# Modulation rows taken in pairs, and queued behind weight products in the first two mixers

## The chip, the cores and the metric

The kernel runs on one core of a Trainium2 chip. The metric is the device time of one execution in microseconds (us); the kernel before takes 1922.84 us, the median of three runs (1920.18 to 1924.93).

## The reference

Four layers run over 256 tokens of width 1024. The first two ("block 1") have a mixer (differential attention with a gated recurrence in the first, dilated attention in the second), a layer norm, a 4096-wide squared-ReLU network and a gate. The last two ("block 2") take the same tokens as a denoising stream beside 256 context tokens: their mixer joins gated linear attention, neighbourhood attention and sliding-window attention. Both are scaled, shifted and gated by six modulation rows for each of the two layers and each of two conditioning vectors. In short, for layer `l`:

```
m = silu([c_2, c_ctx_2]) @ w_mod_2[l] + b_mod_2[l]     # 2 x 6*1024, from 1024 x 6*1024 weights
x = x + m[2] * mixer(rms(x) * (1 + m[1]) + m[0])
x = x + m[5] * ffn  (rms(x) * (1 + m[4]) + m[3])
```

All is float32. The two modulation products read 2 x 25 MB of weights for two rows of output each. They depend on the two conditioning vectors alone, so they can be computed at any time before block 2 uses them.

## The kernel before, in words

Weights stream from HBM on SyncE's queue (SP) in units of up to 512 KB. A unit lands in one of four buffers `wr` (line 212), ScalarE copies it to a rounded high part `wh` (L214) and VectorE takes the rest `wl` (L216). TensorE then makes three products for each weight block: high by high, high by low, low by high (L279 to L281 in projections, L825 to L827 and L850 to L852 in block 1's network, L1473 to L1475 and L1499 to L1501 in block 2's). Each of these is called a weight product here. Units are consumed in the order in which the program names them.

The modulation weights go another way. `modulation(l, box, js)` (L938) makes four parts for each of the six rows `j`; a part `u` covers two blocks of 128 weight rows, `k = 2u` and `2u + 1`. For each block it loads 128 x 1024 numbers (512 KB, L955, SP) into a buffer `raw`, and multiplies them unsplit (L957): `cT`, 128 x 32, is the stationary side, and four products of 256 columns each write one of four groups of 32 partitions of the PSUM tile `fil`, each on its own column group of the array. TensorE runs a float32 product in two passes, so that a block of weight rows has 8 matmul records and a part has 16. In this text a block of weight rows is a **row**, and a part's two rows are a **pair**. VectorE then adds the four groups to `bm` (L959). There is one PSUM buffer `fil`, and there are two buffers for the rows, tag `fr` (the first six rows use `bc`). A row's buffer is free for the next load when its products are done. The whole program has 12 x 4 = 48 pairs.

The list of program items is woven by hand: modulation parts stand between the items of both mixers of block 1 (`mod(0, 0)` to `mod(0, 2)` in the first, `mod(0, 5)` and `mod(1, 0)` in the second), beside the first block of their networks (`mod(0, 3)`, `mod(1, 1)`), in the second network (`mod(0, 4)`), and in block 2. The order on each engine is not that of the list, however. A planner with a timeline of its own goes through the instructions: when an engine comes free in that timeline, the earliest in the list that is ready is queued next, with some evacuations brought forward by `tc.high_priority`. So modulation products can be queued ahead of weight products that stand earlier in the list but aren't ready in the planner's timeline, and other work that becomes ready can be queued between the products of a pair. On the chip each engine takes its queue strictly in that order.

Of the kernel before, what the change touches and what calls it, by code (L numbers as in the profile page):

```python
# [119 lines left out]
def body(ctx: ExitStack, tc: tile.TileContext, A: dict, out: bass.AP):  # L120
# [29 lines left out]

    mm = nc.tensor.matmul
    V = nc.vector
    S = nc.scalar
# [114 lines left out]
    def proj(w, kdim, chunks, xs, evac, t_outer=(), tag="acc", first=0):  # L268
# [6 lines left out]
        def mms(o, x, wt, u):  # L275
            (xh, xl), (wh, wl) = x, wt
            for kk in range(2):
                k = 2 * ((u + first) % nu) + kk
                mm(o, xh[:, k, :], wh[:, kk, :], start=(u == 0 and kk == 0), stop=False)  # L279
                mm(o, xh[:, k, :], wl[:, kk, :], start=False, stop=False)  # L280
                mm(o, xl[:, k, :], wh[:, kk, :], start=False, stop=(u == nu - 1 and kk == 1))  # L281

# [27 lines left out]
    def projT(w, kdim, c0, nb, xs, evac, tag="acc"):  # L310
# [4 lines left out]
        def part(wt, u):  # L315
            (wh, wl), xT = wt, xs.box["T"].both
            if u == 0:
                held.extend(new((P, 2, 256)) for _ in range((nb + 1) // 2))
            for kk in range(2):
                k = 2 * u + kk  # L320
                mh, ml = [m[:, k, :] for m in xT]
                for b in range(nb):
                    o = held[b // 2][:, b % 2, :]
                    bs = slice(b * P, (b + 1) * P)
                    mm(o, wh[:, kk, bs], mh, start=(k == 0 and b % 2 == 0), stop=False, skip_group_check=True)
                    mm(o, wh[:, kk, bs], ml, start=False, stop=False, skip_group_check=True)
                    mm(o, wl[:, kk, bs], mh, start=False, stop=(k == kdim - 1), skip_group_check=True)
            if 2 * u == kdim - 2:
                evac(held)
# [459 lines left out]
    def block1_layer(l, xT, done, side):  # L789
# [25 lines left out]
        def up_part(g, u, wt):  # L815
# [3 lines left out]
            for b in range(4):  # L819
                o = pss[g][b // 2][:, b % 2, :]  # L820
                for kk in range(2):
# [4 lines left out]
                    mm(o, wh[:, kk, bs], ml, start=False, stop=False, skip_group_check=True)  # L826
                    mm(o, wl[:, kk, bs], mh, start=False, stop=(k == 7), skip_group_check=True)  # L827
            if u == 3:
# [9 lines left out]
        def down_part(g, hs, *us):  # L838
# [3 lines left out]
            for t in range(2):  # L842
                ts_ = slice(t * P, (t + 1) * P)
                for n in range(2):
                    o = acc[g][t][n]
                    for i, h in enumerate(hs):
                        wh, wl = us[2 * i + n]
                        for kk in range(2):
                            b = 2 * h + kk
                            mm(o, hh[:, b, ts_], wh[:, kk, :], start=(b == 0), stop=False)  # L850
                            mm(o, hh[:, b, ts_], wl[:, kk, :], start=False, stop=False)  # L851
                            mm(o, hl[:, b, ts_], wh[:, kk, :], start=False, stop=(b == 3))  # L852
                    if 1 in hs:
# [83 lines left out]

    def modulation(l, box, js):  # L938

        st = {}  # L940

        def part(j, u):
# [3 lines left out]
            if u == 0:  # L946
                bm = st[j] = T([P, 256], F32, "gate" if j in (2, 5) else "bm", 3 if j in (2, 5) else 1)
                V.memset(bm, 0.0)
                for s in range(2):
                    nc.sync.dma_start(bm[s:P:32, :], A["b_mod_2"][l, j * D:(j + 1) * D].rearrange("(g n) -> g n", g=4))  # L950
            bm, ps = st[j], PT("fil")
            for k in (2 * u, 2 * u + 1):
                early[0] += 1
                raw = T([P, D], F32, "bc" if early[0] <= 6 else "fr", 2)
                nc.sync.dma_start(raw, A["w_mod_2"][l, k * P:(k + 1) * P, j * D:(j + 1) * D])  # L955
                for g in range(4):
                    mm(ps[32 * g:32 * g + 32, 0:256], cT[:, k, :], raw[:, 256 * g:256 * g + 256],  # L957
                       start=(k == 2 * u), stop=(k == 2 * u + 1), tile_position=(0, 32 * g))
            V.tensor_tensor(bm, ps[:, 0:256], bm, ALU.add)  # L959
# [458 lines left out]
    def block2_layer(l, xT, pr, box, ce, done, side):  # L1418
# [44 lines left out]
        def up_part(g, m, u, wt):  # L1463
# [3 lines left out]
            for b in range(2):  # L1467
                o = pss[g][m][:, b, :]
                bs = slice(b * P, (b + 1) * P)
                for kk in range(4):  # L1470
# [3 lines left out]
                    mm(o, wh[:, kk, bs], ml, start=False, stop=False, skip_group_check=True)  # L1474
                    mm(o, wl[:, kk, bs], mh, start=False, stop=(k == 7), skip_group_check=True)  # L1475
            if m == 1 and u == 1:
# [8 lines left out]
        def down_part(gs, *us):  # L1485
# [5 lines left out]
            for t in range(2):  # L1491
                ts_ = slice(t * P, (t + 1) * P)
                for n in range(2):
                    cs = slice(n * 512, (n + 1) * 512)
                    o = acc["y"][t][n]
                    for i, (g, (hh, hl)) in enumerate(zip(gs, hs)):
                        wh, wl = us[2 * i + n]
                        for kk in range(2):
                            mm(o, hh[:, kk, ts_], wh[:, kk, :], start=(kk == 0 and g == 0), stop=False)  # L1499
                            mm(o, hh[:, kk, ts_], wl[:, kk, :], start=False, stop=False)  # L1500
                            mm(o, hl[:, kk, ts_], wh[:, kk, :], start=False, stop=(kk == 1 and g == NG - 1))  # L1501
                    if NG - 1 in gs:
# [22 lines left out]
    def ctx_ffn(box):  # L1525
# [16 lines left out]
        def up_part(g, m, u, wt):  # L1542
# [3 lines left out]
            for b in range(2):  # L1546
                o = pss[g, m][:, b, :]
                bs = slice(b * P, (b + 1) * P)
                for kk in range(4):
# [3 lines left out]
                    mm(o, wh[:, kk, bs], ml, start=False, stop=False, skip_group_check=True)  # L1553
                    mm(o, wl[:, kk, bs], mh, start=False, stop=(k == 7), skip_group_check=True)
            if u == 0:
# [11 lines left out]
        def down_part(g, *us):  # L1567
# [3 lines left out]
            for t in range(2):  # L1571
                ts_ = slice(t * P, (t + 1) * P)
                for n in range(2):
# [3 lines left out]
                    for kk in range(2):  # L1577
                        mm(o, h[:, 0, kk, ts_], wh[:, kk, :], start=(kk == 0), stop=False)
                        mm(o, h[:, 0, kk, ts_], wl[:, kk, :], start=False, stop=False)
                        mm(o, h[:, 1, kk, ts_], wh[:, kk, :], start=False, stop=(kk == 1))  # L1580
                    if g == 0:
# [79 lines left out]
    program = [do(begin)]  # L1661
    def mod(l, *js):
        return modulation(l, boxes[l], js)

    program += block1_layer(0, xTs[0], to_next(1), dict(tail=flat(ctx_a[:1]), lr=4, mix=mod(0, 0, 1) + ctx_n + mod(0, 2), first=flat(ctx_a[1:2]) + mod(0, 3),
                                                        ffn=ctx_a[2:-2], end=flat(ctx_a[-2:]), last=[]))
    program += block1_layer(1, xTs[1], to_next(2), dict(tail=[], lr=6, mix=mod(0, 5) + mod(1, 0), first=mod(1, 1),
                                                        ffn=weave(ctx_b[:-2], mod(0, 4)), end=flat(ctx_b[-2:]), last=[]))
# [60 lines left out]
```

## Time and profile before

| | us |
|---|---|
| median of three runs | 1922.84 |
| profiled execution | 1921.25 |
| its span | 1919.10 |
| TensorE busy | 1844.6 (96%) |
| VectorE busy | 1224.0 (64%) |
| ScalarE busy | 988.6 (52%) |
| modulation products (L957), union of their time | 64.96 |

The profile's timeline gives an instruction's start, its duration, engine (PE is TensorE, DVE VectorE, ACT ScalarE), line, operands and shape, and how many alike follow each other; in brackets stands the idle time before it and what ended it. `128*32` are the active rows and columns of the array. Matmuls are pipelined, so that the distance of two starts, not the duration, is what one costs. A row of the windows view has the stretch, its length, the busy time with the number of instructions for PE, PEld (weight loads), DVE, ACT and POOL, then the granted TensorE clock as a share of full speed, the mean share of time that the DMA engines were busy, and GB/s. A row of the waits view has who waited, for whom, the total us, how often, and the longest. A row of the chain of waits has start, us, and what the time went to.

### The profile page before, as it was taken

How to read it: one execution, taken by the hardware profiler on the slowest of the kernel's cores; microseconds unless marked ns; L12 is line 12 of the kernel's file. 1: busy time of each engine (PE TensorE's matmuls, PEld its weight loads, DVE VectorE, ACT ScalarE, POOL GpSimd, SP SyncE). 2: the span in 40 equal slices, each digit the busy share in tenths (PEclk: the TensorE clock that was granted, in tenths of full speed). 3: DMA queues.
4: the chain of work that ended last, by engine and by line, in shares of the span. 5: the costliest groups of instructions: out<-in, count | busy, mean ns of one | idle time of the engine just before them, and what ended most of it. 6: DMA issues, size and time to landing. Idle time of an engine off the chain costs nothing. (4 is left out here: it accounts for less than half of the span.)

```text
span 1919.1 us, 31908 instructions
## 1 busy us (share of the span) xinstructions
PE 1844.6 (96%) x12481; PEld 1576.3 (82%) x12481; DVE 1224.0 (64%) x2333; ACT 988.6 (52%) x1630; POOL 50.8 (3%) x74
## 2 busy tenths in 40 slices
PE   7999999999999899999899999999999999989997
PEld 5766888997887688888787889899898886669997
DVE  5565656656676666668577876685646666755555
ACT  5453564544565364544568553454546556344443
POOL 1000000000000000000000000000000000000000
PEclk9999999999999899999899999999999999989999
DMA  8645654545656554465353355556665464456553
GB/s 279 250 165 189 231 183 150 178 156 192 214 171 198 192 188 150 169 220 175 118 170 104 122 162 168 168 181 193 195 212 166 156 187 146 141 176 185 182 183 98
DMA packets 100835, 338.84 MB, mean 177 GB/s; under 512 B 11572, under 2 KB 12812, under 8 KB 100684
## 3 DMA queue, kind: packets, MB, share of 16 engines
q1 hardware_dynamic: 100140, 336.43, 54.5%
q8 instruction: 98, 1.61, 0.4%
q0 software_dynamic: 544, 0.36, 0.2%
q14 instruction: 53, 0.43, 0.1%
HBM read 335.70 MB, written 1.05 MB: 175 GB/s over the span
## 5 line engine op out<-in xcount | busy, mean ns | idle before, releaser
L216 DVE TENSOR_TENSOR wl<-wr,wh 128x1024 fp32r<-128x1024 f32 (+3 forms) x562 | 637.6, 1137 | 412.8 <-ACT wh L214 406.3
L214 ACT CAST wh<-wr 128x1024 fp32r<-128x1024 f32 (+3 forms) x562 | 549.6, 981 | 655.2 <-PE acc L281 132.0
L279 PE MATMUL acc<-wh,mh 128*128 128x256 f32 (+3 forms) x400 | 132.3, 336 | 3.5 <-ACT mh L378 2.0
L280 PE MATMUL acc<-wl,mh 128*128 128x256 f32 (+3 forms) x400 | 130.8, 329 | 0.7 <-DVE wl L216 0.7
L281 PE MATMUL acc<-wh,ml 128*128 128x256 f32 (+3 forms) x400 | 131.1, 330 | 0.0
L279 PE MATMUL acc<-wh,xh 128*128 128x512 f32 (+3 forms) x304 | 117.4, 396 | 6.0 <-ACT xh L378 3.8
L280 PE MATMUL acc<-wl,xh 128*128 128x512 f32 (+3 forms) x304 | 118.6, 390 | 1.7 <-DVE wl L216 1.7
L281 PE MATMUL acc<-wh,xl 128*128 128x512 f32 (+3 forms) x304 | 117.8, 388 | 0.1
L850 PE MATMUL acc<-wh,a 128*128 128x512 f32 x256 | 101.8, 401 | 0.0
L851 PE MATMUL acc<-wl,a 128*128 128x512 f32 x256 | 101.5, 396 | 0.0
L852 PE MATMUL acc<-wh,a 128*128 128x512 f32 x256 | 101.0, 396 | 0.0
L1473 PE MATMUL sc<-xh,wh 128*128 128x256 f32 x352 | 99.7, 284 | 0.5 <-ACT xh L378 0.5
L1474 PE MATMUL sc<-xl,wh 128*128 128x256 f32 x352 | 99.7, 283 | 0.0
L1475 PE MATMUL sc<-xh,wl 128*128 128x256 f32 x352 | 99.5, 283 | 0.0
L1474 PE MATMUL sc<-ml,wh 128*128 128x256 f32 x352 | 99.1, 282 | 0.0
L1473 PE MATMUL sc<-mh,wh 128*128 128x256 f32 x352 | 98.9, 281 | 0.0
L1475 PE MATMUL sc<-mh,wl 128*128 128x256 f32 x352 | 98.4, 280 | 0.0
L279 PEld LDWEIGHTS acc<-wh,mh 128*128 128x128 f32 x400 | 75.3, 189 | 14.2 <-issue 3.2
L280 PEld LDWEIGHTS acc<-wl,mh 128*128 128x128 f32 x400 | 75.8, 189 | 6.6 <-DVE wl L216 1.2
L281 PEld LDWEIGHTS acc<-wh,ml 128*128 128x128 f32 x400 | 75.5, 189 | 6.7 <-issue 0.6
L279 PEld LDWEIGHTS acc<-wh,xh 128*128 128x128 f32 x304 | 58.4, 194 | 22.4 <-ACT xh L378 4.5
L825 PE MATMUL sc<-mh,wh 128*128 128x256 f32 x256 | 74.6, 292 | 1.4 <-DVE ml L358 1.4
(571 smaller groups left out, 4687.1 us busy)
## 6 DMA issues: line engine op xcount, KB each, us to landing
wr<-in_ffn_w_dram SPq DMA_DIRECT2D x128, 512.0 KB
fr<-in_w_mod_dram SPq DMA_DIRECT2D x90, 512.0 KB
wr<-in_w_gate_dram SPq DMA_DIRECT2D x66, 512.0 KB
wr<-in_w_up_dram SPq DMA_DIRECT2D x66, 512.0 KB
wr<-in_w_down_dram SPq DMA_DIRECT2D x66, 512.0 KB
wr<-in_w_in_dram SPq DMA_DIRECT2D x40, 384.0 KB
wr<-in_ev_w_in_dram SPq DMA_DIRECT2D x28, 512.0 KB
wr<-in_w_in_dram SPq DMA_DIRECT2D x28, 512.0 KB
```

The lines of the kernel that those rows point to most:

```text
L214: S.copy(hi, raw)
L216: V.tensor_tensor(lo, raw, hi, ALU.subtract)
L279: mm(o, xh[:, k, :], wh[:, kk, :], start=(u == 0 and kk == 0), stop=False)
L280: mm(o, xh[:, k, :], wl[:, kk, :], start=False, stop=False)
L281: mm(o, xl[:, k, :], wh[:, kk, :], start=False, stop=(u == nu - 1 and kk == 1))
L825: mm(o, wh[:, kk, bs], mh, start=(k == 0 and b % 2 == 0), stop=False, skip_group_check=True)
L850: mm(o, hh[:, b, ts_], wh[:, kk, :], start=(b == 0), stop=False)
L851: mm(o, hh[:, b, ts_], wl[:, kk, :], start=False, stop=False)
L852: mm(o, hl[:, b, ts_], wh[:, kk, :], start=False, stop=(b == 3))
L1473: mm(o, wh[:, kk, bs], mh, start=(k == 0 and b == 0), stop=False, skip_group_check=True)
L1474: mm(o, wh[:, kk, bs], ml, start=False, stop=False, skip_group_check=True)
L1475: mm(o, wl[:, kk, bs], mh, start=False, stop=(k == 7), skip_group_check=True)
```

## The change

`modulation` gets a flag `hold`. A part first allocates and loads both rows of its pair, and then issues its eight products: first each column group with one row (groups 0 and 2 with the second row, 1 and 3 with the first), then each with the other row. With `hold`, the eight products get an edge to the weight product that was traced last before them: TensorE's queue has them behind it, without a wait for its end. `wm` records that product, the third of each triple. All parts of `mod(0, 0)` to `mod(0, 3)`, `mod(0, 5)`, `mod(1, 0)` and `mod(1, 1)` are held (28 pairs); those of `mod(0, 4)` and `mod(1, 2)` to `mod(1, 5)` are not (20 pairs). The row loads, buffers, the number of products and the add on VectorE stay as they are.

```
+    dense = []
+    def wm(*args, **kw):
+        dense[:] = [mm(*args, **kw).ins]
...
-                mm(o, xl[:, k, :], wh[:, kk, :], start=False, stop=(u == nu - 1 and kk == 1))
+                wm(o, xl[:, k, :], wh[:, kk, :], start=False, stop=(u == nu - 1 and kk == 1))
...
-    def modulation(l, box, js):
+    def modulation(l, box, js, hold):
...
+            raws = {}
             for k in (2 * u, 2 * u + 1):
                 early[0] += 1
-                raw = T([P, D], F32, "bc" if early[0] <= 6 else "fr", 2)
-                nc.sync.dma_start(raw, A["w_mod_2"][l, k * P:(k + 1) * P, j * D:(j + 1) * D])
-                for g in range(4):
-                    mm(ps[32 * g:32 * g + 32, 0:256], cT[:, k, :], raw[:, 256 * g:256 * g + 256],
-                       start=(k == 2 * u), stop=(k == 2 * u + 1), tile_position=(0, 32 * g))
+                raws[k] = T([P, D], F32, "bc" if early[0] <= 6 else "fr", 2)
+                nc.sync.dma_start(raws[k], A["w_mod_2"][l, k * P:(k + 1) * P, j * D:(j + 1) * D])
+            with tc.issue_after(dense[0]) if hold and dense else nullcontext():
+                for rnd in range(2):
+                    for g in range(4):
+                        k = 2 * u + (g + rnd + 1) % 2
+                        mm(ps[32 * g:32 * g + 32, 0:256], cT[:, k, :], raws[k][:, 256 * g:256 * g + 256],
+                           start=(k % 2 != g % 2), stop=(k % 2 == g % 2), tile_position=(0, 32 * g))
...
-    program += block1_layer(0, ..., mix=mod(0, 0, 1) + ctx_n + mod(0, 2), first=flat(ctx_a[1:2]) + mod(0, 3), ...
+    program += block1_layer(0, ..., mix=mod(0, 0, 1, hold=True) + ctx_n + mod(0, 2, hold=True), first=flat(ctx_a[1:2]) + mod(0, 3, hold=True), ...
-    program += block1_layer(1, ..., mix=mod(0, 5) + mod(1, 0), first=mod(1, 1), ...
+    program += block1_layer(1, ..., mix=mod(0, 5, hold=True) + mod(1, 0, hold=True), first=mod(1, 1, hold=True), ...
```

The other lines that change from `mm` to `wm` are the third products of the other triples.

## Rows read from the trace of the kernel before

**Rows 1.** The page, part 1: busy time of each engine.
```profile
PE 1844.6 (96%) x12481; PEld 1576.3 (82%) x12481; DVE 1224.0 (64%) x2333; ACT 988.6 (52%) x1630; POOL 50.8 (3%) x74
```

**Rows 2.** Windows over the two mixers of block 1.
```profile
25.00:60.00 35.00, 31.78 (x185) 21.75 (x178) 20.75 (x30) 25.79 (x29) 0.53 (x1) 1.00 0.80 284
...
135.00:162.00 27.00, 24.79 (x178) 16.18 (x177) 15.00 (x45) 8.34 (x25) 0.00 (x0) 0.87 0.69 227
162.00:212.00 50.00, 49.55 (x264) 36.68 (x262) 35.97 (x54) 23.64 (x41) 5.05 (x5) 1.00 0.63 215
...
545.00:615.00 70.00, 68.42 (x562) 53.73 (x561) 47.71 (x200) 40.62 (x117) 0.00 (x0) 0.98 0.64 207
```

**Rows 3.** Source view of line 957, rows in buffers fr: ns min/median/max.
```profile
L957 PE MATMUL fil<-fr,cT x720: 376/379/637, 57.7 to 1867.1; 128*32 128x256 f32 x180
```

**Rows 4.** Timeline of TensorE around a pair taken at once.
```profile
480.17 0.39 PE L281 MATMUL acc<-wh,xl 128*128 128x512 f32 x1
480.49 1.07 PE L957 MATMUL fil<-fr,cT 128*32 128x256 f32 x16
481.49 0.74 PE L279 MATMUL acc<-wh,xh 128*128 128x512 f32 x2
482.07 0.40 PE L280 MATMUL acc<-wl,xh 128*128 128x512 f32 x1
```

**Rows 5.** Timeline of TensorE around a single row.
```profile
42.26 0.39 PE L279 MATMUL acc<-wh,xh 128*128 128x512 f32 x1
42.58 0.64 PE L957 MATMUL fil<-bc,cT 128*32 128x256 f32 x8
43.15 0.50 PE L280 MATMUL acc<-wl,xh 128*128 128x512 f32 x1
43.48 0.39 PE L281 MATMUL acc<-wh,xl 128*128 128x512 f32 x1
```

**Rows 6.** Timeline of TensorE around one product, a quarter of a row.
```profile
645.01 0.39 PE L281 MATMUL acc<-wh,xl 128*128 128x512 f32 x1
645.33 0.62 PE L957 MATMUL fil<-fr,cT 128*32 128x256 f32 x2
645.88 0.50 PE L279 MATMUL acc<-wh,t 128*128 128x512 f32 x1
646.21 0.39 PE L280 MATMUL acc<-wl,t 128*128 128x512 f32 x1
```

**Rows 7.** Timeline of TensorE, further modulation products.
```profile
155.89 1.08 PE L957 MATMUL fil<-fr,cT 128*32 128x256 f32 x8
...
579.26 1.07 PE L957 MATMUL fil<-fr,cT 128*32 128x256 f32 x16
...
596.89 0.62 PE L957 MATMUL fil<-fr,cT 128*32 128x256 f32 x2
```

**Rows 8.** TensorE's waits for modulation rows: 0:212, 466:646 and 1600:1730 us.
```profile
PE fil L957 <- DMA fr<-in_w_mod_dram: 1.0, 1, 1.0
...
PE fil L957 <- DMA fr<-in_w_mod_dram: 1.1, 1, 1.1
...
PE fil L957 <- DMA fr<-in_w_mod_dram: 8.5, 6, 2.9
```

**Rows 9.** Waits of SyncE's queue, the whole span.
```profile
SPq L212 <- DVE wl L216: 1149.4, 432, 18.6
SPq L955 <- PE fil L957: 110.3, 54, 7.9
```

**Rows 10.** Chain of waits in the last layer: a row's landing.
```profile
1702.45 4.73 DMA fr<-in_w_mod_dram
```

**Rows 11.** Timeline of TensorE: the second row of that pair.
```profile
1709.09 1.08 PE L957 MATMUL fil<-fr,cT 128*32 128x256 f32 x8 [0.69 <-DMA fr<-in_w_mod_dram]
```

**Rows 12.** Timelines of VectorE and TensorE at the first layer norm.
```profile
203.72 1.41 DVE L403 SCALAR_TENSOR_TENSOR x<-x,stb,bc 128x512 f32<-128x512 f32 x2
...
206.59 0.66 PE L177 MATMUL sc<-ident,x 128*128 128x128 f32 x4
```

More of the change, by code (lines that the diff above doesn't have):

```diff
@@ L1 @@
 import math
+from contextlib import nullcontext
 from contextlib import ExitStack
@@ L326, in part @@
                     mm(o, wh[:, kk, bs], ml, start=False, stop=False, skip_group_check=True)
-                    mm(o, wl[:, kk, bs], mh, start=False, stop=(k == kdim - 1), skip_group_check=True)
+                    wm(o, wl[:, kk, bs], mh, start=False, stop=(k == kdim - 1), skip_group_check=True)
             if 2 * u == kdim - 2:
@@ L826, in up_part @@
                     mm(o, wh[:, kk, bs], ml, start=False, stop=False, skip_group_check=True)
-                    mm(o, wl[:, kk, bs], mh, start=False, stop=(k == 7), skip_group_check=True)
+                    wm(o, wl[:, kk, bs], mh, start=False, stop=(k == 7), skip_group_check=True)
             if u == 3:
@@ L851, in down_part @@
                             mm(o, hh[:, b, ts_], wl[:, kk, :], start=False, stop=False)
-                            mm(o, hl[:, b, ts_], wh[:, kk, :], start=False, stop=(b == 3))
+                            wm(o, hl[:, b, ts_], wh[:, kk, :], start=False, stop=(b == 3))
                     if 1 in hs:
@@ L1474, in up_part @@
                     mm(o, wh[:, kk, bs], ml, start=False, stop=False, skip_group_check=True)
-                    mm(o, wl[:, kk, bs], mh, start=False, stop=(k == 7), skip_group_check=True)
+                    wm(o, wl[:, kk, bs], mh, start=False, stop=(k == 7), skip_group_check=True)
             if m == 1 and u == 1:
@@ L1500, in down_part @@
                             mm(o, hh[:, kk, ts_], wl[:, kk, :], start=False, stop=False)
-                            mm(o, hl[:, kk, ts_], wh[:, kk, :], start=False, stop=(kk == 1 and g == NG - 1))
+                            wm(o, hl[:, kk, ts_], wh[:, kk, :], start=False, stop=(kk == 1 and g == NG - 1))
                     if NG - 1 in gs:
@@ L1553, in up_part @@
                     mm(o, wh[:, kk, bs], ml, start=False, stop=False, skip_group_check=True)
-                    mm(o, wl[:, kk, bs], mh, start=False, stop=(k == 7), skip_group_check=True)
+                    wm(o, wl[:, kk, bs], mh, start=False, stop=(k == 7), skip_group_check=True)
             if u == 0:
@@ L1579, in down_part @@
                         mm(o, h[:, 0, kk, ts_], wl[:, kk, :], start=False, stop=False)
-                        mm(o, h[:, 1, kk, ts_], wh[:, kk, :], start=False, stop=(kk == 1))
+                        wm(o, h[:, 1, kk, ts_], wh[:, kk, :], start=False, stop=(kk == 1))
                     if g == 0:
@@ L1661, in body, with mod @@
     program = [do(begin)]
-    def mod(l, *js):
-        return modulation(l, boxes[l], js)
-    program += block1_layer(0, xTs[0], to_next(1), dict(tail=flat(ctx_a[:1]), lr=4, mix=mod(0, 0, 1) + ctx_n + mod(0, 2), first=flat(ctx_a[1:2]) + mod(0, 3),
+    def mod(l, *js, hold=False):
+        return modulation(l, boxes[l], js, hold)
+    program += block1_layer(0, xTs[0], to_next(1), dict(tail=flat(ctx_a[:1]), lr=4, mix=mod(0, 0, 1, hold=True) + ctx_n + mod(0, 2, hold=True), first=flat(ctx_a[1:2]) + mod(0, 3, hold=True),
                                                         ffn=ctx_a[2:-2], end=flat(ctx_a[-2:]), last=[]))
-    program += block1_layer(1, xTs[1], to_next(2), dict(tail=[], lr=6, mix=mod(0, 5) + mod(1, 0), first=mod(1, 1),
+    program += block1_layer(1, xTs[1], to_next(2), dict(tail=[], lr=6, mix=mod(0, 5, hold=True) + mod(1, 0, hold=True), first=mod(1, 1, hold=True),
                                                         ffn=weave(ctx_b[:-2], mod(0, 4)), end=flat(ctx_b[-2:]), last=[]))
```

## The prediction

> **What bounds the kernel now.** I read the page's engines first: TensorE is busy for 96% of the span, VectorE for 64%, ScalarE for 52% [rows 1]. So time that is taken out of TensorE's queue counts, unless it lies beside a wait of TensorE. Then the windows over the two mixers of block 1, for how much TensorE idles there: 0.45 of 50 us at 162 to 212 us, 1.6 of 70 at 545 to 615, but 2.2 of 27 at 135 to 162, at a granted clock of 0.87, and 3.2 of 35 at 25 to 60, with the DMA engines 0.80 busy [rows 2]. Then line 957 and TensorE's timeline around it. What the reader is to see there is that modulation products come in **visits**, runs of them between other products, that most visits hold less than a pair, and that a visit's cost hardly depends on how much it holds.
>
> **What a visit costs.** Products of 512 columns normally start 0.23 us apart. Around a whole pair (16 records) the next product starts 1.32 us after the one before (480.17 to 481.49), and two products after it take 0.58 instead of 0.46: 1.32 - 0.23 + 0.12 = 1.21 us [rows 4]. Around one row (8 records) it is 0.89 - 0.23 + 0.10 = 0.76 us [rows 5]. Around a single product (2 records) it is 0.87 - 0.23 + 0.10 = 0.74 us [rows 6]: the four column groups run side by side, so that a quarter of a row takes as long as a row. A visit thus costs 0.31 us for going there and back and 0.45 us for each row that it touches, begun rows counted whole (0.31 + 2 x 0.45 = 1.21).
>
> **How many visits there are.** I counted them by hand in the timeline of line 957 (768 records in all; 720 of them read rows from `fr` [rows 3]). In the part that will be held, 28 pairs are spread over 49 visits with 65 row turns: 20 visits, 25 turns up to 160 us (12 pairs); 7 and 10 at 162 to 212 (4 pairs); 12 and 17 from 467 to 579 (8 pairs; the last is a whole one [rows 7]); 10 and 13 from 597 to 645 (4 pairs, from a visit of one product [rows 7] to another [rows 6]). In the free part 20 pairs stand in 26 visits: 5 for 4 pairs at 712 to 855, 4 for 4 at 1376 to 1494, 12 for 8 at 1620 to 1676 (17 turns), 5 for 4 from 1701 on.
>
> **The change part by part.**
>
> *Pairs.* The number of products, of row loads and of adds stays. The first product of a pair now needs the second row and the second product the first row. If the planner keeps the products to one PSUM tile in their written order, nothing of a pair can be queued until both rows are there in its timeline, and a pair is no longer cut by the landing of its second row. It can still be cut by other work that comes ready.
>
> *Held.* The products can't be queued ahead of weight products that stand earlier in the list. When their turn comes, everything older and dense is queued, they are the oldest work that is ready, and should go in one run. So I count one visit and two turns for each of the 28 pairs: 49 - 28 = 21 visits x 0.31 = 6.5 us, and 65 - 56 = 9 turns x 0.45 = 4.05 us: 10.6 us off TensorE's queue. In the free part the same sum gives 1 x 0.31 at 712 to 855, and 4 x 0.31 + 1 x 0.45 = 1.7 at 1620 to 1676; the latter stretch waits much, so I count a third of it: 0.3 + 0.6 = 0.9.
>
> *Waits for rows.* In the held part TensorE waits twice for a row, 1.0 and 1.1 us [rows 8]. Both are single rows queued before they landed; none of the visits of 16 records shows such a wait. Held pairs come later in the queue, so the bounds are 0 and 2.1 us gained; I take half, 1.0. In the last layer, at 1600 to 1730 us, such waits come to 8.5 us in six [rows 8]. Here a pair's second row decides now. Of two loads issued together at 1702.45 the first landed 4.73 us later [rows 10], and the second held TensorE up until 1709.09 [rows 11], 1.9 us after the first. The bounds are half of the waits gone, -4 us, and each of the 8 pairs before 1676 waiting 1.9 us more, +15 us. I take 0, since the planner will also place the pair later, as it did those of 16 records without a wait.
>
> *Lost cover.* Where a visit lay beside a wait its removal brings nothing. (a) 142 to 160 us holds six single rows, the last two at 1.08 us each instead of 0.64 [rows 7], in the window where TensorE idles and the clock is 0.87 [rows 2]. Merging them saves 3 x 0.31, more at the low clock; all of it, 1.1 us, I take to fall into the idle time beside it. (b) The four pairs of `mod(0, 3)` now stand behind the network's first weight products, after the first layer norm. Before, visits at 199 and 206 us (1.21 + 0.66 us) lay before its transposes, which start at 206.59 while VectorE had the row ready at 203.72 + 1.41 = 205.13 [rows 12]: 1.46 us of slack, so 0.4 us shows, and about 0.8 us more before the second tile's: 1.2 us. (c) In the tail of the second mixer (600 to 616 us) three visits of 2.7 us lie between attention steps; bounds 0 and 2.7, I take 1.3.
>
> *The queues.* The row loads themselves are not held, but a row's buffer comes free later when its products do. SyncE waits 110.3 us in all for line 957's buffers, with the weight loads behind it in the same queue; those wait 1149.4 us for VectorE to free theirs [rows 9], which is slack that such a shift has to use up first. I cost it at nothing; if the cover were gone, one more wait of the longest kind, 7.9 us, bounds it. VectorE's 48 adds stay, and free the one `fil` bank sooner when a pair isn't cut.
>
> **A rule that speaks against it.** The window 135 to 162 shows a clock of 0.87, that is a quarter of it, 7.0 us, at the lower of the two levels (1.2 instead of 2.4 GHz), and in the profile's clock that follows stretches in which TensorE did little [rows 2]. The Trainium skill, "TensorE: Matmul & The Clock Gate", section "HAM oscillation — how this bites in real kernels", says that gaps between bursts of matmuls throttle the array again; by it, taking filler out of the mixers' tails would cost clock. One more stretch like this one would cost half of 7.0, 3.5 us, and the sum would be 5.4 us instead of 8.9.
>
> **Sum.** 10.6 + 0.9 + 1.0 - 1.1 - 1.2 - 1.3 = 8.9 us. The profiled execution, 1921.25 (span 1919.10 and 2.15 around it), goes to 1912.3; it lies 1.6 us under the median of 1922.84, so the forecast is **1914 us**.
>
> **Rivals.**
>
> 1. *Rows land too late (slower).* In the last layer each of 8 pairs waits 1.9 us longer for its second row, 15 us: 1914 + 15 = 1929. For it: the chain of waits runs through row loads there [rows 10]. Against: visits of 16 records wait for none. It decides from where row waits in that stretch pass 8.5 + 8.9 = 17.4 us: then the rest is eaten.
> 2. *The pairs don't stay whole (the change doesn't do what it says).* If the planner queues groups 1 and 3 on the first row and the rest on the second, a cut pair has one turn and then two, instead of one and one: 0.45 us more for each. If 21 are cut as before, 9.5 us: 1922.8 + 9.5 = 1932.
> 3. *The saved time falls beside waits (no change).* Merges inside both mixers bring nothing, since weights or attention steps come no sooner, and only the row turns of the stretches where TensorE never waits are saved. The early window at 0.80 of DMA time speaks for it [rows 2], the 0.45 us of idle time in 50 against. About half of the sum, 4.5 us: 1918.5.
>
> **How the numbers follow.** A measurement of this kernel tells a change from none from about 0.3%, 5.8 us. Forecast 0.54; rival 1 0.12, rival 2 0.08, rival 3 0.26. The forecast and a little of rival 3 are faster by more than 5.8 us: 0.55. The rest of rival 3 and the near side of rival 1 are within it: 0.28. The far sides of rivals 1 and 2 are slower: 0.17. Low end: nothing lost to cover, both waits gone, the free merges whole and half of the last layer's waits gone: 10.6 + 2.0 + 2.1 + 4.2 = 18.9, so 1904. High end: rival 1, 1929. The forecast's own range is 1908 to 1918.
>
> **What would show it.** Right: in the timeline line 957 has about 28 visits before 650 us, nearly all of 16 records at 1.07 us, and some 20 after; `mod(0, 3)` and `mod(1, 1)` stand after their layer norms, among the network's products. Lost cover shows as waits of TensorE for VectorE or ScalarE at the layer norms and in the attention tail of the second mixer; rival 1 as row waits over 8.5 us between 1600 and 1730; rival 2 as visits of 4 records followed by 12. What would make it wrong: the planner makes a new order for everything after the first moved product, and a stretch that has nothing to do with modulation could gain or lose some us by that.

## The result: 1945.28 us, 1.2% slower, and the profile after

The kernel after takes 1945.28 us (median; 1941.81 to 1948.55) against 1921.84 (1920.18 to 1924.93) for the kernel before, run beside it: a ratio of 1.0118 [1.0102, 1.0135], 23.4 us slower. 1914 was forecast, with a range from 1904 to 1929. The profiled execution has a span of 1942.4 us. Its lines stand 7 later than before up to L950 and 12 later from there on (L957 is now L969, L177 is L184, L1229 is L1241).

The page, part 1, and the source view of the modulation products:

```profile
PE 1846.2 (95%) x12481; PEld 1585.5 (82%) x12481; DVE 1225.8 (63%) x2333; ACT 989.9 (51%) x1630; POOL 52.6 (3%) x74
```
```profile
L969 PE MATMUL fil<-fr,cT x720: 376/379/636, 58.0 to 1890.2; 128*32 128x256 f32 x180
```

The same 12481 products take 1.6 us more of TensorE's time [rows 1], and TensorE stands idle for 96.2 us instead of 74.5 (span less busy time): 21.7 of the 23.3 us by which the span grew. The visits did become fewer. Counted as before, the held pairs stand in 32 visits instead of 49 and the free ones in 22 instead of 26; 44 of the 54 hold 16 records, and 40 of these take 1.07 us:

```profile
572.15 0.62 PE L969 MATMUL fil<-fr,cT 128*32 128x256 f32 x2
...
670.91 1.07 PE L969 MATMUL fil<-fr,cT 128*32 128x256 f32 x16
```

That saving is eaten by TensorE's clock. The profile's clock records sum to 78.2 us at the lower level (1.2 GHz) before and 108.8 after; 58.8 and 83.3 us of these lie under busy products. By estimate, 24.5 us more at half speed are 12.3 us of extra time. The stretches at the lower level that grew most are 467 to 477 us, at the boundary between the two layers (10.2 us, before 3.4), 610 to 621, in the second mixer's tail (10.2, before 3.4), and 709 to 720, at the start of the second network (10.2, before none). The windows show them, first after, then before (columns as in [rows 2]):

```profile
466.00:485.00 19.00, 15.89 (x52) 11.46 (x51) 3.79 (x7) 7.38 (x18) 0.55 (x1) 0.73 0.25 80
...
600.00:640.00 40.00, 38.80 (x217) 28.11 (x216) 23.15 (x67) 18.52 (x43) 0.00 (x0) 0.87 0.46 160
...
700.00:720.00 20.00, 14.91 (x65) 11.94 (x64) 13.24 (x28) 9.15 (x20) 0.00 (x0) 0.74 0.45 155
```
```profile
466.00:485.00 19.00, 16.98 (x89) 11.78 (x90) 6.80 (x12) 9.07 (x21) 0.55 (x1) 0.91 0.53 181
...
600.00:640.00 40.00, 38.42 (x240) 27.08 (x239) 23.64 (x61) 18.26 (x44) 0.00 (x0) 0.96 0.55 185
...
700.00:720.00 20.00, 20.00 (x153) 16.96 (x152) 12.73 (x25) 11.07 (x22) 0.00 (x0) 1.00 0.57 190
```

In the tail of the first mixer TensorE idles 3.1 and 2.6 us more than in [rows 2], at the same clock as before:

```profile
135.00:162.00 27.00, 21.66 (x142) 16.02 (x141) 13.15 (x38) 10.47 (x33) 1.25 (x2) 0.87 0.52 179
162.00:212.00 50.00, 46.93 (x238) 36.07 (x237) 36.77 (x51) 23.58 (x37) 4.32 (x4) 1.00 0.61 200
```

**The bank.** TensorE's timeline shows why it waits at 700 us, first before, then after (idle time and its releaser in brackets):

```profile
651.50 0.38 PE L177 MATMUL fil<-ident,cgy 128*128 128x128 f32 x2
...
655.22 0.38 PE L177 MATMUL fil<-ident,cgy 128*128 128x128 f32 x2
658.80 1.97 PE L177 MATMUL sc<-ident,x 128*128 128x128 f32 x8 [3.20 <-DVE ml L358]
660.70 1.22 PE L1229 MATMUL fil<-ck,c 64*128 64x256 f32 x2
```
```profile
661.47 1.77 PE L184 MATMUL sc<-ident,x 128*128 128x128 f32 x8 [3.42 <-DVE ml L365]
665.65 0.58 PE L832 MATMUL sc<-mh,wh 128*128 128x256 f32 x1 [2.41 <-DVE ml L365]
...
705.91 0.38 PE L184 MATMUL fil<-ident,cgy 128*128 128x128 f32 x2
...
709.15 0.44 PE L184 MATMUL fil<-ident,cgy 128*128 128x128 f32 x2 [2.85 <-DVE xl L365]
710.51 1.22 PE L1241 MATMUL fil<-ck,c 64*128 64x256 f32 x2 [0.92 <-DVE xl L365]
713.04 0.79 PE L1241 MATMUL sm<-ck,c 64*128 64x256 f32 x1 [1.32 <-ACT t L1261]
```

The context stream transposes its recurrence's output `cgy` into the one `fil` bank, splits it, and starts its attention scores in the same bank. Before, that short serial chain lay at 651 to 661 us, in the gap of the second layer norm, where TensorE waits anyway. Now `mod(1, 1)`, earlier in the list, is held behind the second network's first weight products, from 671 us on. Its tiles come before `cgy`'s in the list, the bank is handed out in the list's order (all its 148 users are issued in that order in both kernels), and so the chain starts 54 us later, alone: its steps now leave TensorE idle for 2.85, 0.92 and 1.32 us, and the clock falls behind them.

**The rows.** TensorE's waits for modulation rows, in the stretches of [rows 8] (0:212, and 1615:1745, where the stretch of the last layer now lies):

```profile
PE fil L969 <- DMA fr<-in_w_mod_dram: 3.8, 2, 2.9
```
```profile
PE fil L969 <- DMA fr<-in_w_mod_dram: 10.5, 4, 4.6
```

They are fewer and longer. At 466:646 there is none.

### The profile page after: what moved, and what is told of

It is laid out like the page before. It is cut to its first block, busy times and chain, and to the rows that moved or that the text cites. A ratio compares the mean times of both kernels' runs of the same rounds, so it can differ in the third digit from the quotient of the medians.

```text
span 1942.4 us, 31901 instructions
## 1 busy us (share of the span) xinstructions
PE 1846.2 (95%) x12481; PEld 1585.5 (82%) x12481; DVE 1225.8 (63%) x2333; ACT 989.9 (51%) x1630; POOL 52.6 (3%) x74
## 5 line engine op out<-in xcount | busy, mean ns | idle before, releaser
L157 PE MATMUL acc<-wh,a 128*128 128x512 f32 x472 | 186.5, 396 | 0.0
L157 PE MATMUL sc<-xh,wl 128*128 128x256 f32 x608 | 172.7, 284 | 0.0
L157 PE MATMUL sc<-mh,wl 128*128 128x256 f32 x608 | 171.4, 283 | 0.0
L157 PEld LDWEIGHTS sc<-xh,wl 128*128 128x128 f32 x608 | 117.4, 193 | 0.1
L157 PEld LDWEIGHTS sc<-mh,wl 128*128 128x128 f32 x608 | 115.6, 190 | 1.4 <-issue 1.4
L157 PEld LDWEIGHTS acc<-wh,a 128*128 128x128 f32 x472 | 89.0, 188 | 21.8 <-issue 0.4
L857 PE MATMUL acc<-wh,a 128*128 128x512 f32 x256 | 102.0, 402 | 0.0
L1485 PE MATMUL sc<-mh,wh 128*128 128x256 f32 x352 | 98.9, 281 | 0.0
```

The costliest lines, as they stand in the source:

```text
L157: dense[:] = [mm(*args, **kw).ins]
L1485: mm(o, wh[:, kk, bs], mh, start=(k == 0 and b == 0), stop=False, skip_group_check=True)
```

## Experiments

Three theories. **T1**: a held pair blocks every later user of `fil`, in the list's order. **T2**: in the last layer, where rows come late, a pair waits until both of its rows have landed. **T3**: held rows no longer fill gaps of TensorE, and stand in dense stretches instead. Since many stretches jitter with the clock, I read two lengths of each trace beside the time: from the start to the end of block 1's second network (VectorE's seventh BATCH_NORM_AGGREGATE, L397 before), and the rest. "Network 2" is the stretch to that point from VectorE's fifth update of `x` at L859 before. Each ratio is to the kernel before, run beside it. The lengths are those of one profiled execution, which lies up to 8.2 us from its kernel's median (R 1943.62, Q 1921.64, A 1931.7), and kernels with the same order of instructions up to the end of network 2 differ there by 5 us (E against A, L against F). So they tell where time goes better than how much.

| kernel | time | ratio to before | to end of network 2 | rest | network 2 |
|---|---|---|---|---|---|
| before (profile) | 1921.25 | | 882.5 | 1036.6 | 186.1 |
| after | 1945.28 | 1.0118 [1.0102, 1.0135] | 898.3 | 1044.1 | 196.0 |
| A pairs, no hold | 1939.15 | 1.0096 [1.0059, 1.0133] | 881.5 | 1048.4 | 186.1 |
| B hold, single rows | 1936.18 | 1.0083 [1.0057, 1.0109] | 898.2 | 1036.5 | 192.9 |
| C after, (1, 1) free | 1940.15 | 1.0092 [1.006, 1.0125] | 891.7 | 1047.0 | 186.1 |
| D after, (1, 1) listed later | 1942.16 | 1.0116 [1.0093, 1.0138] | 886.9 | 1056.2 | 189.2 |
| E pairs but not in last layer | 1928.12 | 1.0029 [1.0003, 1.0056] | 886.1 | 1037.2 | 186.1 |
| F as E, (0, 0) to (0, 2), (1, 0) held | 1924.1 | 1.0012 [0.9998, 1.0027] | 892.3 | 1034.9 | 186.1 |
| G pairs in last layer alone | 1932.34 | 1.0035 [1.0013, 1.0057] | 881.4 | 1043.3 | 186.1 |
| H hold (1, 1) alone | 1926.46 | 1.0017 [1.0002, 1.0032] | 886.9 | 1040.8 | 192.9 |
| I before, four row buffers | 1932.28 | 1.0052 [1.0028, 1.0075] | 883.7 | 1045.4 | 186.1 |
| J as G, four row buffers | 1933.41 | 1.0061 [1.0037, 1.0084] | 880.7 | 1048.6 | 186.1 |
| K hold (0, 5) alone | 1920.22 | 0.9992 [0.9977, 1.0006] | 885.2 | 1037.3 | 186.1 |
| L as F, all pairs, four buffers | 1935.2 | 1.0067 [1.0042, 1.0091] | 887.3 | 1046.1 | 186.1 |
| M as G, one load for a pair | 1923.43 | 1.0003 [0.9984, 1.0023] | 882.2 | 1037.7 | 186.1 |
| N before, one load for a pair | 1923.57 | 1.0002 [0.9989, 1.0015] | 882.9 | 1040.0 | 186.1 |
| O hold (0, 0) to (0, 2) alone | 1924.18 | 1.0003 [0.9985, 1.0021] | 885.0 | 1038.5 | 186.0 |
| P hold (1, 0) alone | 1926.74 | 1.0022 [1.0006, 1.0038] | 888.0 | 1034.8 | 186.1 |
| Q hold (0, 3) alone | 1927.13 | 1.0024 [1.001, 1.0038] | 882.7 | 1036.8 | 186.1 |
| R hold (0, 5), (1, 0), (1, 1) | 1935.47 | 1.0075 [1.0057, 1.0094] | 902.4 | 1039.1 | 193.0 |

From E on, `modulation` takes two lists that say which rows `(l, j)` are held and which paired; each edit is these lists.

**A and B: the two halves of the change.**

```
A  -        return modulation(l, boxes[l], js, hold)
   +        return modulation(l, boxes[l], js, False)
B  each row loaded, then multiplied by itself as before, inside `with tc.issue_after(dense[0]) if hold ...`
```

> Rows in pairs as in the change, but no pair is held. Theory 1 (bank queue): the single PSUM bank fil is handed out in list order, so that a held pair holds up everything that comes behind it for fil, the context stream above all; without the hold the 15.7 us that the changed kernel has lost by its first unheld pair (728.04 against 712.51 us) come back, and only the 7 to 8 us that it lost after 1620 us stay: 1929 us or less. Theory 2 (both rows must have landed before a pair's first product): nothing changes, 1945 us. Theory 3 (the held pairs no longer fill the gaps of the layer norms, and nothing else does): as theory 1 in time, 1929.

> The hold as in the change, but each row with its own four products, as before. Theory 1 and theory 3: the 15.7 us of the held part stay, the 7 to 8 us after 1620 us come back: about 1938 us. Theory 2: back to the kernel before, 1922 us.

The table splits the loss by place. B has all of it up to the end of network 2 (898.2, as after), and none behind; A has none there and 11.8 us in the rest. The two times don't multiply to the whole: 1.0096 x 1.0083 is 1.0180, not 1.0118. Free pairs also save visits (40 instead of 49 up to 700 us), but TensorE's idle time up to 882 us goes from 30.8 to 38.9, and nothing of the saving is seen.

**C, D and H: `mod(1, 1)` and the bank.**

```
C  -        first=mod(1, 1, hold=True),
   +        first=mod(1, 1),
D  -        first=mod(1, 1, hold=True), ffn=weave(ctx_b[:-2], mod(0, 4))
   +        first=[], ffn=weave(ctx_b[:-2], mod(1, 1, hold=True) + mod(0, 4))
H  HOLD, PAIR = [(1, 1)], []
```

> The whole change, but the four pairs of mod(1, 1) are not held. Theory 1: the context stream's first transposes and scores, which now stand at 706 to 714 us with 5.1 us of waits and 10.2 us at half clock, go back into the layer norm's gap at 650 us; 10 to 14 us come back, 1931 to 1935 us. Theory 2: 1945. Theory 3: the layer norm's gap is filled again with these pairs, 5 to 10 us come back, and the context stream moves too, so that this run doesn't separate it from theory 1.

> The whole change, with mod(1, 1) still held, but listed behind the start of the context attention, woven with it and with mod(0, 4). In the order of fil the context's transposes now come before these pairs. Theory 1: the context start goes back into the gap at 650 us and the stretch at 706 to 714 loses its waits, 8 to 12 us come back, 1933 to 1937. Theory 3: the pairs still don't fill the gap, so that at most 3 us come back, 1942 to 1946. Theory 2: 1945.

> The kernel before, with the four pairs of mod(1, 1) held, as single rows, and nothing else changed. Theory 1: the context's transposes go from 651 us to after the last of these rows, near 700, with a wait of 2.9 us, and the stage from the first add of the second network's last half to its layer norm, 186 us before, takes 193 to 196; the whole about 1930. Theory 3 (only the gap at the layer norm is lost): idle time of the stage before it grows by 3 us or more, that stage stays at 186, the whole 1925.

The stretch itself answers for T1. Network 2 takes 186.0 or 186.1 us in every kernel in which `mod(1, 1)` isn't held, 192.9 to 193.0 when its single rows are, and 196.0 when its pairs are. What is added is waiting and clock: TensorE idles there for 4.2 us in B, H and R, for 5.1 in the kernel after and not at all in the fifteen in which `mod(1, 1)` isn't held, and the records at the lower clock sum to 6.8, 10.2 and 0 us. In D, where the context's scores come first again, both are 0:

```profile
642.71 0.44 PE L184 MATMUL fil<-ident,cgy 128*128 128x128 f32 x2
...
651.09 1.01 PE L1241 MATMUL fil<-ck,c 64*128 64x256 f32 x2
```

In D `mod(1, 1)` still costs time there, but no wait. How much, its 189.2 us understates, since D's seventh aggregate comes 7.4 us before its eighth, where 1.2 us lie between them before and after: up to TensorE's last product of the network it is 188.7 us in D, 182.0 before and 191.9 after. H has the waits of the bank with no pairs and no other hold (640:735):

```profile
PE sc L184 <- DVE x L410: 3.5, 1, 3.5
PE fil L1246 <- DVE xl L365: 2.8, 1, 2.8
PE sc L184 <- DVE ml L365: 2.6, 1, 2.6
PE sm L1246 <- ACT t L1266: 1.3, 1, 1.3
```

So T1 is shown for this place: with `mod(1, 1)` held, and listed ahead of the context's start, network 2 is 6.8 to 9.9 us longer. The totals that I expected of C and D failed: 5.1 us came back instead of 10 to 14, and 3.1 instead of 8 to 12. In D the last layer takes back what the bank gave: between the products of L1499 and L1500 (lines of before) of the third layer and those of the fourth lie 251.4 us, in the kernel after 241.4, before 234.6. TensorE idles there as long as in the kernel after (27.2 and 27.4 us), but the records at the lower clock sum to 54.6 us instead of 27.3, by estimate 13.7 us of time. Why they do is open.

**K, O, P, Q and R: the other holds.** `HOLD` is the list in the table, `PAIR` empty.

> Before with only mod(0, 5) held, single rows. T3 (held rows leave the gap between the layers, where they cost nothing, and stand in the dense mixer instead): the stretch from the gate to the layer's start loses rows but not time (56.1 within 1 us), the mixer grows by 3 to 5 us, +3 to +6 us in all: 1925 to 1928. T1 (what a held row blocks costs, not its place): nothing is queued behind these rows for `fil`, so no change, within 2 us.

> Before with only mod(0, 0) to mod(0, 2) held (the first mixer's twelve pairs), single rows. The whole of the holds with single rows cost 16 us up to the end of the second network (882 us before); mod(1, 1) alone 4.8 and mod(0, 5) alone 3 of these. T3 (filler taken from gaps): half of the remaining 8 us here, 1924 to 1928. T1 (nothing else uses `fil` behind these rows but their own adds): no loss, within 2 us of before.

> Before with only mod(1, 0) held (the second mixer's tail, four pairs, beside which no stream of the context uses `fil`). T1: no loss, within 2 us of before. T3: the tail of the second mixer and the layer norm after it lose filler, 2 to 5 us more, with TensorE idle in 600 to 660 us.

> Before with only mod(0, 3) held, single rows (the four pairs beside the first block of the first network). The holds alone so far: first mixer 1.0003, mod(0, 5) 0.9992, mod(1, 0) 1.0022, mod(1, 1) 1.0017; their sum is 6.5 us of the 16 that all holds cost together with single rows. If the pieces add, mod(0, 3) carries up to 9 us of the rest, 1928 to 1932, with the layer norm before the first network idle for longer. If not, within 2 us of before, and the rest comes from holds acting together.

> Before with mod(0, 5), mod(1, 0) and mod(1, 1) held together, single rows: every held row that stands in the second layer's mixer and network. If the pieces add, 0.9992 x 1.0022 x 1.0017 = 1.0031, 1928. If holds act together (the later rows are pushed on by the earlier ones, so that none is left for the layer norm's gap and mod(1, 1) stands in the bank's way for longer), 1934 to 1938, as with all holds (1936.2), and the stretch from the second network's layer norm to its end is 190 to 193 + 69 us as there.

Alone, the holds cost little: O 0.0003, K -0.0008, P 0.0022, Q 0.0024 and H 0.0017, which is 11 us together where B has 16; by the intervals that is no clear difference. P's 4.2 us are within the 2 to 5 that T3 gave it; O and K, which cost nothing that can be told, speak for T1. The three of the second layer together (R) cost 14.4 us instead of the 6 of their sum, and that difference is clear. R's waits at 636:720 are those of the kernel after, the bank's among them:

```profile
PE sc L184 <- DVE ml L365: 3.4, 1, 3.4
...
PE fil L1246 <- DVE xl L365: 2.8, 1, 2.8
PE sc L832 <- DVE ml L365: 2.2, 1, 2.2
PE sm L1246 <- ACT t L1266: 1.3, 1, 1.3
```

What differs is what the holds push on. In H alone, moving `mod(1, 1)` out shortens the second mixer (120.9 us instead of 126.4, from VectorE's fourth instruction of L918 to its fifth update of `x` at L802, lines of before; six traces with the order of before have 124.9 to 130.2). That pays for about half of what it costs later, 3.8 us from there to network 2 and 6.8 in it. In R `mod(0, 5)` has left the boundary and stands in that mixer (128.8 us): nothing is paid back, and the layer norm stands open (73.1 us instead of 64.8 from there to network 2; 69.5 in B and after). That fits T3 for the holds together, but it is argued: no run fills one gap by itself. Of (0, 5) alone, where I had put 3 to 6 us on it, T3 failed.

**E, F, G: pairs, in and out of the last layer.**

```
E  HOLD, PAIR = [], [(0, 0), ..., (0, 5), (1, 0), (1, 1), (1, 2)]
F  HOLD, PAIR = [(0, 0), (0, 1), (0, 2), (1, 0)], [(0, 0), ..., (0, 5), (1, 0), (1, 1), (1, 2)]
G  HOLD, PAIR = [], [(1, 3), (1, 4), (1, 5)]
```

> Pairs everywhere but in the last layer, where mod(1, 3) to mod(1, 5) take single rows again; nothing held. Theory 2 for the last layer (a pair waits for both rows, TensorE idles long enough to drop its clock): from 1227 us on it runs as the kernel before, and the block 1 stages as in the run with pairs alone, 0 to 4 us ahead: 1918 to 1922 us. Rival (pairing costs by the new order it gives everywhere): 1930 or more.

> As the run before this one (pairs, but single rows in the last layer), with mod(0, 0) to mod(0, 2) and mod(1, 0) held, whose parts lie inside the mixers, and mod(0, 3), mod(0, 5) and mod(1, 1), which lay over layer boundaries, free. Theory 1 (a held part does harm where it keeps fil from the context stream or leaves a boundary's gap empty): no loss, 1917 to 1922 us. Rival (any hold costs in its place, by about half of the 15 us that holding alone cost): 1927 to 1930.

> The kernel before, with pairs in the last layer alone (mod(1, 3) to mod(1, 5)), nothing held. Theory 2 for the last layer: row waits of TensorE after 1590 us go from 8.5 to about 10 us in fewer, longer ones of 3 to 4.6 us, the half clock there from 31 to 40 us or more, together 8 to 20 us: 1930 to 1941. Rival (the loss after 1227 us comes from what the change did before): 1921.

E missed: 1918 to 1922 was expected, and free pairs outside the last layer cost 0.0029, with an interval that begins at 0.0003. None of the three theories says why. F, with some of these pairs held, lies 2.3 us above before, with 1 in its interval.

That pairs in the last layer cost time is clear. The rest is 1034.8 to 1040.8 us (mean 1037.3) in the ten kernels that have two buffers, both loads and single rows in the last layer, and 1043.3 to 1056.2 (mean 1047.8) in the five with pairs there. In the last layer's stretch, as measured for D, TensorE idles 18.8 to 23.2 us in the ten and 26.6 to 27.5 in the five; its row waits are 0.2 to 8.5 and 9.7 to 10.9. The chain of waits of G shows two of these waits (start, us, what), and SyncE's queue their loads:

```profile
1653.72 1.00 PE fil L974 x16
...
1655.19 5.24 DMA fr<-in_w_mod_dram
...
1662.01 4.50 DMA fr<-in_w_mod_dram
```
```profile
1654.77 0.81 SPq L963 DMA_DIRECT2D fr<-in_w_mod_dram  x2
1661.59 0.80 SPq L963 DMA_DIRECT2D fr<-in_w_mod_dram  x2
```

A pair ends at 1654.72; at 1654.77 both buffers are free and both loads are issued; they land more than 5 us later, and only then can the next pair run. Two buffers that a pair fills both are one buffer. But the kernel before, with single rows in the same two buffers, has such pieces in its chain too:

```profile
1659.85 3.77 DMA fr<-in_w_mod_dram
...
1664.44 3.69 DMA fr<-in_w_mod_dram
```

Over 1615:1745 they are 15.8% of its chain and 16.5% of G's. Other work covers part of each: TensorE itself idles there for 2.94 and 1.14 us before, and for 2.50 and 2.26 in G:

```profile
1663.75 0.64 PE L957 MATMUL fil<-fr,cT 128*32 128x256 f32 x8 [2.94 <-DMA fr<-in_w_mod_dram]
...
1668.27 0.64 PE L957 MATMUL fil<-fr,cT 128*32 128x256 f32 x8 [1.14 <-DMA fr<-in_w_mod_dram]
```
```profile
1660.47 1.07 PE L974 MATMUL fil<-fr,cT 128*32 128x256 f32 x16 [2.50 <-DMA fr<-in_w_mod_dram]
...
1666.65 1.94 PE L974 MATMUL fil<-fr,cT 128*32 128x256 f32 x16 [2.26 <-DMA fr<-in_w_mod_dram]
```

Against before, row waits make 2.4 of the 6.2 us that TensorE idles longer in G. The waits for VectorE's attention tiles `mx` and `t` make 2.7 and 1.5 more (1506:1750, first before, then G):

```profile
PE sc L1229 <- DVE mx L1242: 3.0, 2, 2.1
...
PE sm L177 <- DVE t L1256: 2.0, 1, 2.0
```
```profile
PE fil L974 <- DMA fr<-in_w_mod_dram: 10.9, 5, 4.3
PE sc L1246 <- DVE mx L1259: 5.7, 3, 3.5
PE sm L184 <- DVE t L1273: 3.5, 2, 2.0
```

So T2 fits, but the load time alone doesn't carry the loss; the new order of the attention around the pairs is a rival. G's ratio times B's, 1.0035 x 1.0083, is the 1.0118 of the whole change; that is partly luck, since pairs outside the last layer have a price of their own (E, 1.0029), and with it the product is 1.0148.

**I, J, L, M, N: is it the buffers?**

```
I, J  -  raw = T([P, D], F32, "bc" if early[0] <= 6 else "fr", 2)
      +  raw = T([P, D], F32, "bc" if early[0] <= 6 or (l == 1 and j in (3, 4) and u % 2) else "fr", 2)
L     HOLD, PAIR = [(0, 0), (0, 1), (0, 2), (1, 0)], [all twelve]; buffers as J
M, N  +  if l == 1 and j > 2 and k % 2:
      +      raws[k] = raws[k - 1]
      +  else: (allocate and load as before)
```

> The kernel before, with the odd parts of mod(1, 3) and mod(1, 4) in the two buffers `bc` (shared there with the attention tile pTs) instead of `fr`: four buffers instead of two for these 16 rows. Theory T2 (in the last layer rows are late because a load starts only when a buffer is free and lands some 5 us later): the row waits of 10.5 us in 1615 to 1745 fall to under 3, l2(1) mixer 462.8 goes to 455 to 461, total 2 to 8 us below before. Rival (the waits there are the planner's order, or the shared `bc` delays pTs): row waits as before, total within 3 us or slower.

> Before with pairs in mod(1, 3) to mod(1, 5) alone (as the run that paired only the last layer, 1932.3) and four buffers for mod(1, 3) and mod(1, 4). T2 as sharpened: a pair frees both of its buffers at its end, so with two buffers the whole load time of some 5 us stands between two pairs; with four the next pair's rows land while this one waits for its turn. Then row waits go from 10.9 to under 3 us, half clock in the l2(1) mixer to under 12 us, and the time to 1918 to 1926. Rival (pairs block the bank `fil` there, whatever the rows do): waits for rows go, others take their place, 1928 to 1934.

> All pairs; held only in mod(0, 0) to mod(0, 2) and mod(1, 0), where nothing else uses `fil` behind them; four buffers for mod(1, 3) and mod(1, 4). If T1, T2 and T3 together are the cause of the loss, what is left is the gain of the visits: block 1 as in the run with these holds (1924.1) and the last layer as in the run with pairs and four buffers: 1914 to 1922. If pairs cost for another reason, 1926 or more.

> Before with pairs in mod(1, 3) to mod(1, 5) alone, but there only the even row of each pair is loaded and is multiplied twice (the odd rows' share of these three modulation rows is left out; products, adds and their number stay). Now a pair waits for one load and holds one of the two buffers. T2 (the loss from pairs in the last layer is the load time between two pairs, since both buffers come free only at a pair's end): row waits of 10.9 us fall to under 3, and the time is the same as, or up to 4 us below, that of the same omission with single rows. Rival (pairs there cost by their place in the order, or by what waits for the bank): 5 to 10 us above the same omission with single rows, as with both loads (1932.3 against 1922).

> The kernel before with the same omission: in mod(1, 3) to mod(1, 5) only the even row of each pair is loaded, and multiplied twice. It is what the run with pairs and one load is compared with. T2: the row waits of 8.5 to 10.5 us in the last layer fall to under 3 us and the time by 5 to 10 us, to 1912 to 1917. Rival: the waits are replaced by others (as with more buffers), 1919 to 1924.

Four buffers took J's row waits away and brought nothing for the time; I's row waits stayed (8.2 us, before 8.5). The first rows are J's waits at 1615:1750, the second those of its SyncE queue at 1600:1700:

```profile
PE sc L184 <- DVE a L1013: 7.9, 2, 4.7
...
PE fil L974 <- DMA fr<-in_w_mod_dram: 1.9, 1, 1.9
...
PE fil L974 <- DMA bc<-in_w_mod_dram: 1.8, 3, 0.7
```
```profile
SPq L963 <- DVE bc L1289: 25.0, 3, 13.6
...
SPq L963 <- PE acc L1302: 16.2, 5, 7.0
```

The row waits fall from G's 10.9 us to 3.7, but TensorE idles in that stretch as long as in G (27.5 and 27.4 us): the two borrowed buffers `bc` belong to the attention, and SyncE's queue now waits 25.0 us for VectorE's use of them and 16.2 for TensorE's. I, with single rows, is slower too; its queue waits 9.6 us for TensorE's use of them. So J didn't decide, and L, meant to collect the gain of the visits, carried the price of the borrowed buffers along (rest 1046.1).

M and N need no further buffer: they load one row for a pair and multiply it twice, which leaves out the odd rows' share of these three modulation rows. Then the row waits are 1.0 and 1.1 us, and M (1923.43) takes as long as N (1923.57). That does not decide either. With one row to wait for, the planner cuts M's pairs up again, just as it cuts N's rows (visits of 4, 10 and 6 records in both): by line and tile, VectorE's, ScalarE's and GpSimd's instructions come in the same order in both, and TensorE's but for two of 12481. On the engines they are nearly one kernel. What they show is that G's 0.35% needs the second load, either by its wait or because only that keeps a pair together. T2 remains argued. N also shows that the 8.5 us of row waits before [rows 8] were worth nothing: nearly without them the time is that of before.

## Why the prediction was wrong

- **The visits: right in kind, 1.8 us off.** At the prediction's own prices, 17 + 4 visits and some 7 row turns saved are 21 x 0.31 + 7 x 0.45 = 9.7 us, where 11.5 was forecast: 32 held visits came about instead of 28. Rival 2, pairs that don't stay whole, is out.
- **Held: the step that failed.** The forecast followed held products to where they go (the oldest ready work, one run) and asked what they would save. It did not ask who stands behind them for the `fil` bank. "The queues" looked at SyncE's queue and VectorE's adds, and named the bank only as coming free sooner; the queue that mattered is that of a PSUM tag with one buffer, in the list's order. Its price is 6.8 to 9.9 us in network 2. All holds together cost 16 us (B), and those of the second layer alone 14.4 (R).
- **Lost cover: the places were too few.** Priced were the first mixer's tail, the first layer norm and the second mixer's tail, 3.6 us. In the first layer the visits saved and the cover lost balance: VectorE's third aggregate comes at 448.1 us after and at 445.1 to 450.5 in the ten traces with the order of before up to there. What was left out is the boundary at 466 to 485, where `mod(0, 5)`'s first visits had stood (5 visits at 467.39 to 503.10 before, none after; from the third aggregate to the fourth instruction of L918 it is 55.9 us, before 56.1, so that taking them away saved nothing), and the second layer norm, whose waits for VectorE's `ml` grew from 3.20 + 1.39 to 3.42 + 2.41 us, now with no transposes of `cgy` between them.
- **The clock: right in kind, wrong in size.** One more stretch at 1.2 GHz was weighed, 3.5 us, and left out of the sum. The records show 30.6 us more of it, by estimate 12.3 us of extra time. The Trainium skill, "TensorE: Matmul & The Clock Gate", section "HAM oscillation — how this bites in real kernels", had said that gaps between bursts throttle the array again; the windows at 0.73 and 0.74 agree, with gaps of 0.5 to 1.6 and of 0.9 to 2.9 us.
- **The last layer: the second step that failed.** 0 was taken for its row waits, and nothing else was priced there. The row waits grew by only 2.0 us (8.5 to 10.5), but the rest of the program took 7.5 us more, and with pairs TensorE idles there some 6 us longer (G 27.4, before 21.2). The sum had no term for the other waits; the prediction's last sentence named their likely source, a new order of the planner, without a price. Rival 1 had the place and the sign, but its own mark, 17.4 us of row waits, was not reached. How much of the loss is load time and how much the new order stays open. The Trainium skill, "Trainium Kernel Development and Optimization", section "Best Practices", asks for double buffers so that transfers overlap with compute; here they overlap in part, with 2.50 and 2.26 us of TensorE's idle time left in G and 2.94 and 1.14 before.
- **The held rows' waits: wrong way.** 1.0 us was to be gained; these waits went from 2.1 us to 3.8 [rows 8].
- **Rival 3** fits where holds are absent: of A's fewer visits nothing is left up to 882 us, where TensorE idles 8.1 us longer.

The two failed steps, 16 us (B) and 7 (G), are of one size with the 23 us of the result, with the reservation made at G. Open are the clock in D's last layer and why E's free pairs cost time. That `mod(0, 3)`, by its time 0.0024, doesn't show in Q's lengths is no riddle: Q's profiled execution, 1921.64, lies 5.5 us under its median.

## What to carry to other kernels

An order forced on one engine is forced on everything that shares a buffer with the forced work: before an instruction is held back, list the later users of its PSUM tag, and see where they stood. A step that takes both of two buffers has no load under way while it runs, as G's chain shows; before it is made larger, price that, and the new order of the work around it. Filler was worth most here where the engine would stand still, also by what it did for the clock; taken from there to save its fixed cost, it lost both.

## What the runs showed that was not expected

The same program's time moves with the clock it is granted, by more than many of the effects here: A came to 1931.7 and 1934.63 us at a mean clock of 0.977, and to 1943.67 and 1944.58 at 0.971 and 0.972. Network 2 is 186.0 to 186.1 us in the fifteen traces in which TensorE never idles there and `mod(1, 1)` isn't held. Differences below some 5 us are thus better read from such stretches than from the whole.
